# Gated GELU on one core: blocks of 16 rows with one packed store in place of tiles of 8 rows

## The chip, the cores and the metric

The kernel runs on one core of a Trainium2 chip. The metric is the device time of one execution in microseconds; the median of three runs before the change is 469.12 us (469.11 to 469.23). The profile is of one further execution, whose span from the first to the last instruction is 467.9 us.

## The reference

```python
def reference(x):                       # x: (32, 512, 2048) float32
    half_dim = x.shape[-1] // 2
    x1, x2 = x[..., :half_dim], x[..., half_dim:]
    gelu_x1 = 0.5 * x1 * (1 + erf(x1 / np.sqrt(2)))
    return (gelu_x1 * x2).astype(np.float32)
```

There are 16,384 rows. Each is 8 KB in and 4 KB out: 134.22 MB are read and 67.11 MB are written.

## The kernel before

The rows are cut into 16 tiles of 1024 rows. A tile gives every one of the 128 partitions 8 consecutive rows (R = 8), so that a partition's part is 64 KB of input that lies together in memory and 32 KB of output that lies together. Two input buffers (`x0_tile`, `x1_tile`, 64 KB per partition each) and two output buffers (`o0_tile`, `o1_tile`, 32 KB each) alternate by tile: tile i uses number i % 2.

Four engines take part, each with a program of its own, in order:
- SyncE (SP) issues the loads (`load`, L47). Three are issued ahead: tile 0 in two pieces of four rows and tile 1 whole. In the loop it waits until tile i is multiplied (L108) and then issues the load of tile i + 2 into the buffer that tile i has left (L109).
- ScalarE (ACT) waits for the tile (L79), applies GELU to the first halves of the rows (L81) into the output buffer, and issues the store (`store`, L51, the DMA at L54) after a wait for the multiply. The store goes into ScalarE's own DMA queue (q10); the loads go into SyncE's (q1).
- VectorE (DVE) multiplies the output buffer by the second halves of the rows, in place (L89).
- GpSimd sets four constants at the start, TensorE does nothing.

A full tile is computed in two steps of 5 and 3 rows; the first and the last tile in steps of 2, 2 and 4 rows, with a store for each four rows. The semaphore `ready[k]` counts both the load and the store of buffer pair k: ScalarE starts tile i + 2 when the load of it has landed and the store of tile i has as well. The last three stores (tile 14, and two halves of tile 15) go through SyncE's queue, behind the last load. At the end the semaphores are cleared, and SyncE waits for the last stores.

A DMA's work is shared by 16 DMA engines. Transfers of one queue are taken in order; the two queues are served by the same 16 engines.

Of the kernel before, what the change touches and what calls it, by code (L numbers as in the profile page):

```python
# [1 line left out]

# [4 lines left out]

GELU = mybir.ActivationFunctionType.Gelu


@with_exitstack
def kernel(
    ctx: ExitStack,
    tc: tile.TileContext,
    x: bass.AP,
    out: bass.AP,
):
    nc = tc.nc
    P = nc.NUM_PARTITIONS

    x_flat = x.flatten_outer_dims()
    out_flat = out.flatten_outer_dims()
    n_rows, dim = x_flat.shape
    half = dim // 2

    R = 8
    x_t = x_flat.rearrange("(n p r) d -> n p r d", p=P, r=R)
    o_t = out_flat.rearrange("(n p r) d -> n p r d", p=P, r=R)
    n_tiles = x_t.shape[0]
    x_bufs = [nc.alloc_sbuf_tensor(f"x{k}_tile", [P, R, dim], x.dtype) for k in range(2)]  # L30
    o_bufs = [nc.alloc_sbuf_tensor(f"o{k}_tile", [P, R, half], out.dtype) for k in range(2)]

    first = [nc.alloc_semaphore(f"first{j}") for j in range(2)]
    ready = [nc.alloc_semaphore(f"ready{k}") for k in range(2)]
    gelu_done = nc.alloc_semaphore("gelu_done")
    mul_done = nc.alloc_semaphore("mul_done")
    tail_stored = nc.alloc_semaphore("tail_stored")
    n = {sem.name: 0 for sem in [*first, *ready, gelu_done, mul_done, tail_stored]}  # L40

    def counted(ins, sem, by):
        ins.then_inc(sem, by)
        n[sem.name] += by

    def load(i, rows, sem):
        ins = nc.sync.dma_start(out=x_bufs[i % 2][:, rows, :], in_=x_t[i][:, rows, :])  # L47
        counted(ins, sem, 16)
        return ins

    def store(queue, i, rows, sem):  # L51
        queue.wait_ge(mul_done, n[mul_done.name])
        counted(
            queue.dma_start(out=o_t[i][:, rows, :], in_=o_bufs[i % 2][:, rows, :]), sem, 16  # L54
        )

    for ins in (  # L60
        load(0, slice(0, 4), first[0]),
        load(0, slice(4, 8), first[1]),
        load(1, slice(0, 8), ready[1]),
    ):
        tc.no_tile_sem_insts.add(ins.ins.name)
    tc.close()
    tc.compile()  # L67

    for i in range(n_tiles):
        k = i % 2  # L70
        last = i == n_tiles - 1
        pieces = i == 0 or last
        steps = ((0, 2), (2, 4), (4, 8)) if pieces else ((0, 5), (5, 8))
        for lo, hi in steps:
            rows = slice(lo, hi)
            if i == 0 and lo % 4 == 0:
                nc.scalar.wait_ge(first[lo // 4], 16)
            elif lo == 0:
                nc.scalar.wait_ge(ready[k], n[ready[k].name])  # L79
            counted(  # L80
                nc.scalar.activation(  # L81
                    out=o_bufs[k][:, rows, :], in_=x_bufs[k][:, rows, :half], func=GELU
                ),
                gelu_done,
                1,
            )
            nc.vector.wait_ge(gelu_done, n[gelu_done.name])
            counted(
                nc.vector.tensor_mul(  # L89
                    out=o_bufs[k][:, rows, :],  # L90
                    in0=o_bufs[k][:, rows, :],
                    in1=x_bufs[k][:, rows, half:],
                ),
                mul_done,
                1,
            )
            if pieces and hi % 4 == 0:
                if last:
                    store(nc.sync, i, slice(hi - 4, hi), tail_stored)
                else:  # L100
                    store(nc.scalar, i, slice(hi - 4, hi), ready[k])
        if not pieces:
            if i == n_tiles - 2:
                store(nc.sync, i, slice(0, R), tail_stored)
            else:
                store(nc.scalar, i, slice(0, R), ready[k])
        if i + 2 < n_tiles:
            nc.sync.wait_ge(mul_done, n[mul_done.name])  # L108
            load(i + 2, slice(0, R), ready[k])  # L109


    nc.scalar.drain()  # L112
    for sem in (*first, *ready):
        nc.scalar.sem_clear(sem)
    nc.vector.drain()
    nc.vector.sem_clear(gelu_done)
    nc.sync.sem_clear(mul_done)
    nc.sync.wait_ge(tail_stored, n[tail_stored.name]).then_inc(
        tail_stored, -n[tail_stored.name]
    )  # L120


# [1 line left out]
_INS = ['x']  # L124
_OUTS = [((32, 512, 1024), 'float32')]


# [23 lines left out]
```

## Time and profile before

| what | value |
|---|---|
| median of three runs | 469.12 us |
| span of the profiled execution | 467.9 us |
| VectorE busy, 34 multiplies | 140.5 us (30%) |
| ScalarE busy, 34 GELUs and a table load | 115.5 us (25%) |
| GELU of 5 rows (128x5120), 3 rows (128x3072) | 4.47 us, 2.75 us |
| multiply of 5 rows, 3 rows | 5.49 us, 3.35 us |
| mean rate of the DMA over the span | 430 GB/s |

The page's row of DMA shares divides the span into 40 slices of 11.7 us; a digit is the share in tenths in which the 16 engines were busy in a slice. The DMA section counts packets, megabytes and the share of the engines' time for each queue; q1 is SyncE's, q10 ScalarE's. "DMA issues" gives the median time from issue to landing, which includes the time that a transfer stands in its queue. The chain of waits is followed back from the last instruction: at each step to the work that released it. Windows are stretches of the span, in microseconds from its start, for which the packets that begin in them are counted.

### The profile page before, as it was taken

Reading aid. Unit: us, or ns where it says so; the run is one execution under the profiler, and the core shown is the slowest. Engines: PE = TensorE matmul, PEld = TensorE weight load, DVE = VectorE, ACT = ScalarE, POOL = GpSimd, SP = SyncE. Lnnn points to the kernel's source line nnn. Section 1 sums busy time; section 2 is a strip of 40 time slices with the busy share of each in tenths; the row PEclk is TensorE's granted clock in tenths of the full one; section 3 lists DMA queues with packets and bytes.
Section 4 is the critical chain, followed back from the end, with each engine's and each line's share of the span. In section 5 each row is a group of like instructions: output and inputs, shape, how many; then the busy total and the mean of one; then the engine's idle time right before and its main releaser. Section 6 shows DMA issues by size and latency. Waiting matters only on the chain.

```text
span 467.9 us, 152 instructions
## 1 busy us (share of the span) xinstructions
DVE 140.5 (30%) x34; ACT 115.5 (25%) x35; POOL 0.2 (0%) x4
## 2 busy tenths in 40 slices
DVE  0330514207052060511606116060150702507043
ACT  1320606042060410604106050050500506014060
POOL 0000000000000000000000000000000000000000
DMA  8999999999999999999999999999999999999998
GB/s 359 448 448 443 403 405 492 409 403 448 459 437 403 434 417 493 403 403 448 476 420 403 445 406 493 403 406 445 487 409 403 445 451 448 403 434 417 493 389 373
DMA packets 5041, 201.34 MB, mean 430 GB/s; under 512 B 560, under 2 KB 560, under 8 KB 560
## 3 DMA queue, kind: packets, MB, share of 16 engines
q1 hardware_dynamic: 2880, 142.61, 70.6%
q10 hardware_dynamic: 2160, 58.72, 29.1%
q14 instruction: 1, 0.01, 0.0%
HBM read 134.22 MB, written 67.11 MB: 430 GB/s over the span
## 4 chain that ended last, share of the span: by engine, by line
DMA 76%; DVE 14%; ACT 8%; ACTq 0%; SPq 0%; issue 0%
DMA out_dram<-o_tile 66%; DVE o_tile L89 14%; DMA x_tile<-in_x_dram 10%; ACT o_tile L81 8%; ACTq L112 0%; SPq L47 0%
## 5 line engine op out<-in xcount | busy, mean ns | idle before, releaser
L89 DVE TENSOR_TENSOR o_tile<-o_tile,x_tile 128x5120 f32<-128x5120 f32 (+3 forms) x34 | 140.5, 4171 | 319.7 <-ACT o_tile L81 319.7
L81 ACT ACTIVATE o_tile<-x_tile 128x5120 f32<-128x5120 f32 (+3 forms) x34 | 114.3, 3407 | 337.4 <-DMA out_dram<-o_tile 301.6
L81 ACT ACT_TABLE_LOAD x1 | 1.3, 1283 | 2.9 <-PEq L67 2.9
L135 POOL MEMSET const-bfloat16-1.0<- 128x1 bf16 x1 | 0.1, 101 | 0.0
L135 POOL MEMSET const-uint8-127<- 128x1 uint8 x1 | 0.1, 101 | 0.0
L135 POOL MEMSET const-float32-0.0<- 128x1 f32 x1 | 0.1, 98 | 0.2 <-issue 0.2
L135 POOL MEMSET const-float32-1.0<- 128x1 f32 x1 | 0.1, 98 | 0.0
## 6 DMA issues: line engine op xcount, KB each, us to landing
out_dram<-o_tile ACTq DMA_DIRECT2D x13, 4096.0 KB, 44.7
x_tile<-in_x_dram SPq DMA_DIRECT2D x2, 4096.0 KB, 16.6
out_dram<-o_tile ACTq DMA_DIRECT2D x2, 2048.0 KB, 34.5
out_dram<-o_tile SPq DMA_DIRECT2D x1, 4096.0 KB, 25.2
out_dram<-o_tile SPq DMA_DIRECT2D x2, 2048.0 KB, 7.8
x_tile<-in_x_dram SPq DMA_DIRECT2D x15, 44.2
```

What stands on the lines that cost most here:

```text
L81: nc.scalar.activation(out=o_bufs[k][:, rows, :], in_=x_bufs[k][:, rows, :half], func=GELU),
L89: nc.vector.tensor_mul(out=o_bufs[k][:, rows, :], in0=o_bufs[k][:, rows, :], in1=x_bufs[k][:, rows, half:],),
L135: nc = _bacc.Bacc("TRN2", target_bir_lowering=False, num_devices=1)
```

## The change

The unit of work becomes a block of 16 rows per partition, in two halves of 8 rows; there are 8 blocks. For a partition, a half is one load of 64 KB, and the block's output is one store of 64 KB.

There are three buffers of 64 KB per partition in place of four. The first halves alternate in `x0_tile` and `x1_tile` (`buffer_of`), all second halves use `x2_tile`. GELU is computed in place in the input buffer. The multiply writes packed rows of 4 KB into the first half's buffer: the results of the first half into its lower 32 KB, those of the second half into its upper 32 KB. VectorE waits for its own previous multiply before each one.

The order of the loads: (0,0), (0,1) and (1,0) are issued ahead, all whole. When block b is multiplied, ScalarE issues its store and SyncE issues load (b+1, 1) into `x2_tile`. Then SyncE waits until the store of block b has landed (`stored`) and issues load (b+2, 0) into the buffer that was stored. The semaphores `landed` count loads only. All halves are computed in steps of 5 and 3 rows, except for the very last, which keeps 2, 2 and 4. The last block is stored in three pieces through SyncE's queue: 8 rows, 4 rows, 4 rows. There are 16 loads and 10 stores where there were 17 and 18.

```diff
-    x_t = x_flat.rearrange("(n p r) d -> n p r d", p=P, r=R)
-    o_t = out_flat.rearrange("(n p r) d -> n p r d", p=P, r=R)
-    x_bufs = [nc.alloc_sbuf_tensor(f"x{k}_tile", [P, R, dim], x.dtype) for k in range(2)]
-    o_bufs = [nc.alloc_sbuf_tensor(f"o{k}_tile", [P, R, half], out.dtype) for k in range(2)]
+    x_t = x_flat.rearrange("(n p h r) d -> n h p r d", p=P, r=R, h=2)
+    o_t = out_flat.rearrange("(n p r) d -> n p r d", p=P, r=2 * R)
+    bufs = [nc.alloc_sbuf_tensor(f"x{k}_tile", [P, R * dim], x.dtype) for k in range(3)]
...
+    def buffer_of(b, h):
+        return 2 if h else b % 2
+
+    def load(b, h):
+        k = buffer_of(b, h)
+        dst = bufs[k][:, :].rearrange("p (r d) -> p r d", r=R)
+        return counted(nc.sync.dma_start(out=dst, in_=x_t[b, h]), landed[k], 16)
+
+    def packed(b, lo, hi):
+        rows = bufs[b % 2][:, lo * half : hi * half]
+        return rows.rearrange("p (r d) -> p r d", d=half)
+
+    def store(queue, b, lo, hi, sem):
         queue.wait_ge(mul_done, n[mul_done.name])
+        counted(queue.dma_start(out=o_t[b][:, lo:hi, :], in_=packed(b, lo, hi)), sem, 16)
+
+    def compute(b, h, lo, hi):
+        src = bufs[buffer_of(b, h)][:, lo * dim : hi * dim]
+        src = src.rearrange("p (r d) -> p r d", d=dim)
         counted(
+            nc.scalar.activation(out=src[:, :, :half], in_=src[:, :, :half], func=GELU),
+            gelu_done,
+            1,
+        )
+        if n[mul_done.name]:
+            nc.vector.wait_ge(mul_done, n[mul_done.name])
+        nc.vector.wait_ge(gelu_done, n[gelu_done.name])
+        counted(
+            nc.vector.tensor_mul(
+                out=packed(b, h * R + lo, h * R + hi),
+                in0=src[:, :, :half],
+                in1=src[:, :, half:],
+            ),
+            mul_done,
+            1,
         )
...
+    for ins in (load(0, 0), load(0, 1), load(1, 0)):
         tc.no_tile_sem_insts.add(ins.ins.name)
...
+    for b in range(n_blocks):
+        last = b == n_blocks - 1
+        for h in range(2):
+            k = buffer_of(b, h)
+            waited[k] += 16
+            nc.scalar.wait_ge(landed[k], waited[k])
+            if last and h:
+                for lo, hi in ((0, 2), (2, 4), (4, 8)):
+                    compute(b, h, lo, hi)
+                    if hi % 4 == 0:
+                        store(nc.sync, b, R + hi - 4, R + hi, tail_stored)
+            else:
+                for lo, hi in ((0, 5), (5, 8)):
+                    compute(b, h, lo, hi)
                 if last:
+                    store(nc.sync, b, 0, R, tail_stored)
+        if last:
+            continue
+        store(nc.scalar, b, 0, 2 * R, stored[b % 2])
+        nc.sync.wait_ge(mul_done, n[mul_done.name])
+        load(b + 1, 1)
+        if b + 2 < n_blocks:
+            nc.sync.wait_ge(stored[b % 2], n[stored[b % 2].name])
+            load(b + 2, 0)
...
+    for sem in stored:
+        nc.sync.wait_ge(sem, n[sem.name])
+        nc.sync.sem_clear(sem)
```

## The prediction

> **What bounds the kernel now.** I read the page first: the row of DMA shares, then the packet counts and the two queues.
>
> ```profile
> DMA  8999999999999999999999999999999999999998
> ...
> DMA packets 5041, 201.34 MB, mean 430 GB/s; under 512 B 560, under 2 KB 560, under 8 KB 560
> ...
> q1 hardware_dynamic: 2880, 142.61, 70.6%
> q10 hardware_dynamic: 2160, 58.72, 29.1%
> ```
>
> The 16 DMA engines are busy for 70.6 + 29.1 = 99.7% of the span. VectorE (30%) and ScalarE (25%) are far from it. The counts say how a transfer is cut. q1 is SyncE's queue and holds 20 transfers (17 loads, 3 stores at the end); 2880 / 20 = 144 packets: 128 with data, one per partition, and 16 small ones. q10 is ScalarE's: 15 stores, 2160 / 15 = 144. A full load is 8.39 MB, so its packets are 64 KB; a full store's are 32 KB.
>
> Next the chain that ended last, in order of time, for one tile of the steady part:
>
> ```profile
> 100.56 4.48 ACT o_tile L81
> ...
> 105.06 8.77 DVE o_tile L89 x2
> ...
> 113.85 44.68 DMA out_dram<-o_tile
> ...
> 158.56 4.48 ACT o_tile L81
> ```
>
> The same buffer comes round every 158.56 - 100.56 = 58.00 us, in which two tiles move 2 x 12.58 MB: 433.9 GB/s. So 8.39 MB alone takes 19.33 us and a 64 KB packet, 1/8 of it on each engine, 2.42 us. From landing to issue the chain takes 13.3 us (4.48 + 8.77 + handovers); the DMA does not notice, since the other buffer's load and store are queued.
>
> The issues show how the two queues share an engine:
>
> ```profile
> out_dram<-o_tile ACTq DMA_DIRECT2D x13, 4096.0 KB, 44.7
> ...
> x_tile<-in_x_dram SPq DMA_DIRECT2D x15, 44.2
> ```
>
> A store of half the bytes, issued with a load, lands with it. So the queues take turns packet by packet, 32 KB against 64 KB.
>
> Last, how soon a queue that was empty is served. The first load's issue starts at 0.73 (timeline); up to 1.73 no packet has run, up to 2.31 all 16 engines have their first: 1.0 to 1.6 us. The first store is issued at 19.23:
>
> ```profile
> 19.23 0.38 ACTq L54 DMA_DIRECT2D out_dram<-o_tile  x1
> ```
>
> Packets in the window 19.2 to 24.3, then in 19.2 to 25.05:
>
> ```profile
> DMA packets 63, 2.06 MB, mean 405 GB/s; under 512 B 16, under 2 KB 16, under 8 KB 16
> ...
> q1 hardware_dynamic: 63, 2.06, 99.1%
> ```
>
> ```profile
> q1 hardware_dynamic: 66, 2.26, 94.5%
> q10 hardware_dynamic: 16, 0.26, 10.4%
> ```
>
> For 5 us only loads run. If the store was visible after 1.0 to 1.6 us (20.2 to 20.8), then beside the packet in progress each engine still passed the load's small packet (all 16 lie between 21.58 and 22.08) and one whole packet of the next load. I read this as about two packets committed ahead. It is the reading that decides this case.
>
> **The change, part by part.**
>
> *Fewer packets.* 35 transfers become 26, so each engine handles 81 packets fewer (9 each). The first half-load, 8 packets of 32 KB, took 22.46 - 12.76 = 9.70 us between landings; six times that is 58.20, with 54 packets against the 36 of a 58.00 us period for the same bytes: 0.20 / 18 = 0.011 us a packet at most, given rounding. 81 x 0.011 = 0.9; the other end is 0. I take 0.4 us gained.
>
> *Start.* The two 32 KB-row loads of tile 0 become one, and the early GELU at 12.76 moves to 22.46. Cost 0: three 8.39 MB loads stand in SyncE's queue and keep the engines busy until 22.08 + 2 x 19.33 = 60.7. Without that cover it would cost the 9.7 us.
>
> *Compute.* In-place GELU with a strided output, packed multiply: strided input is there already (5120 columns 4.47 us, VectorE 5.49). I take 0; the other bound is VectorE's 23% higher time for its strided form, some 3 us on 13.3. VectorE's new wait on its own last multiply loses the overlap of the pair, 5.49 + 3.35 - 8.77 = 0.07, about 0.1 us. Both lie under the load in flight (below).
>
> *Tail.* From the last landing, 448.56, to the end, 19.3 us: same three stores, same queue, same pieces. Two waits of SyncE on `stored` precede its last wait and lie under the last store. Cost 0.
>
> *The moved load.* SyncE now waits for `stored[b % 2]` before the load of the next first half, and before the multiply wait and load behind it. Call X the first-half load in flight, S the block's store, Y the second-half load issued with S, Z the first-half load that waits for S. ScalarE's own queue holds nothing urgent: the next GELU needs X. Block 0 from the rows:
> - Load (0,0) seen 22.46; (0,1) at 41.8; S and Y issued at 41.8 + 13.4 = 55.2. X's packets end at 60.2 to 60.7, so on the first engine its seventh runs 55.4 to 57.8, its eighth to 60.2.
> - S is visible at 56.2 to 56.8, in the seventh packet. With two packets committed, the eighth and X's small one pass; S starts at 60.2.
> - S and Y have 8 packets each, now of one size, and alternate: both end at 60.2 + 16 x 2.42 = 98.9. Then **both queues are empty**, and Z is issued only when S is seen.
>
> The price of an empty queue: the first load took 12.0 us from issue to landing, of which 4.19 MB account for 9.67: 2.35 us of overhead. With the 0.02 us handover, 2.37 us idle.
>
> Block 1: Y seen at 99.75, S and Y issued 113.1. Z, now X, started late and has its last packets end at 120.6; at 114.1 its sixth packet runs, the seventh and eighth are committed, S comes before X's small packet, which takes a turn. So Y has one packet, 2.42 us, left when S's small packet goes. Z needs 0.4 to be seen by the last engine, up to 0.5 of spread, 1.0 to its first packet: 1.9 to 2.0. No idle time. Z follows Y directly, as in block 0. So the gap comes at every second handover: 3 of the 6 (Z exists for blocks 0 to 5).
>
> Sum against the profiled execution: 467.9 - 0.4 + 3 x 2.37 = 474.6 us. The median lies 1.2 us above the span (469.12), so 475.8.
>
> A rule against this reading: the Trainium skill, "DMA: Bandwidth & Descriptors", section "Queues, rings and completion order", says that an engine drains a whole packet, typically 9 to 17 descriptors, before it turns to the other queue. An engine's share of a transfer here is 9 pieces, so by the rule S would run whole between X and Y, Z would find Y still queued, and the time would be 468.7. The trace disagrees: between 131 and 157.5 us q1 ran 112 packets and q10 122, interleaved, and the store lands with the load.
>
> **Rivals.**
> 1. *No idle time: 467.5 + 1.2 = 468.7 us, not slower.* If S takes its turn right after X's seventh or eighth packet, as the 1.0 to 1.6 us of the first load would have it, one or two packets of Y (2.4 to 4.8 us) are left at each handover, over the 2.0 needed. It decides as soon as fewer than two packets are committed ahead. For it: the first store is one event, and on a queue that had never run. Against it: all 16 engines show those 5 us alike.
> 2. *A gap at all six handovers: 467.5 + 6 x 2.37 = 481.7, median 482.9.* It takes one more committed packet, or a chain from landing to issue longer by a packet (the 3 us bound on compute). For it: the margin in odd blocks is only 2.42 - 2.0 = 0.4 us. Against it: with a third packet committed the first store would have come one packet later than it did if it was visible at 20.8, and the compute forms hardly differ.
> 3. *The larger store packets speed the transfers up.* At the most 0.9 us: 467.0 + 1.2 = 468.2. The queues already run at 433.9 GB/s; there is nothing else to win.
>
> **How the numbers follow.** Forecast (three gaps) 0.38, all six 0.21, none 0.36 with the 0.9 us end in it, other slow phases between them 0.05. A difference under 0.2% (0.9 us) can't be told from none here. Slower: 0.38 + 0.21 + 0.05 = 0.64; within: 0.34; faster: 0.02, only the upper end of the packet gain. Time 475.8. The forecast's own range is 474 to 478 (gap 1.9 to 3 us each); for 8 in 10 it must reach the no-gap case below, 468.4, and the six-gap case above, 483.5.
>
> **What would show it.** Right: DMA digits of 7 or 8 in the slices around 99, 217 and 336 us (2.4 us of 11.9), and GB/s near 350 there; q1 2736 packets, q10 1008. A small packet of a store that comes with the small packet of Y means gap; ahead of Y's last data packet means none. All nines: rival 1. Six dips: rival 2. Wrong altogether if the GELU or multiply rows grow by more than 1 us, or if 1:1 phases run off 434 GB/s.

## The result, and the profile after

The median of six runs is 492.47 us against 469.28 us for the kernel before: 4.9% longer. The runs of the kernel after spread from 486.5 to 497.4 us where those before stay within 0.3 us; the ratio with its interval, 1.0439 (1.0408 to 1.0470), compares only runs near a kernel's fastest and so lies below that of the medians. The profiled execution took 493.68 us, with a span of 492.4 us: 24.5 us more than before. The forecast was 475.8 us, with 468.4 to 483.5 as the range: the direction was right, the size under a third of what came.

The page of the kernel after, the same rows as before, and the issues:

```profile
DMA  9999999999999999999999999999999999999978
...
DMA packets 3745, 201.34 MB, mean 409 GB/s; under 512 B 416, under 2 KB 416, under 8 KB 416
...
q1 hardware_dynamic: 2736, 142.61, 70.4%
q10 hardware_dynamic: 1008, 58.72, 27.8%
...
x_tile<-in_x_dram SPq DMA_DIRECT2D x16, 43.4
out_dram<-x_tile ACTq DMA_DIRECT2D x7, 43.9
```

The packet counts are those worked out. But the digits hide the loss: the engines are busy for 70.4 + 27.8 = 98.2% of a span that is 24.5 us longer, and move 409 GB/s in place of 430. 98.2% of 492.4 us is 17.0 us more busy time than 99.7% of 467.9 us. So most of the lost time is not idle time of the DMA engines; it is packets that take longer.

Windows from one start of the second half's GELU to the next, one per block, then the end. The columns are the stretch, its length, VectorE's, ScalarE's and GpSimd's busy time, the clock, the DMA share and GB/s:

```profile
41.86:101.57 59.71, 17.70 (x4) 14.24 (x4) 0.00 (x0) 1.00 1.00 421
101.57:161.66 60.09, 17.70 (x4) 14.24 (x4) 0.00 (x0) 1.00 0.99 419
161.66:221.74 60.08, 17.70 (x4) 14.25 (x5) 0.00 (x0) 1.00 1.00 418
221.74:282.27 60.53, 17.70 (x4) 14.24 (x4) 0.00 (x0) 1.00 0.99 417
282.27:342.70 60.43, 17.70 (x4) 14.24 (x5) 0.00 (x0) 1.00 0.99 415
342.70:404.43 61.73, 17.70 (x4) 14.24 (x4) 0.00 (x0) 1.00 0.99 415
404.43:472.96 68.53, 17.70 (x4) 14.25 (x5) 0.00 (x0) 1.00 0.97 380
472.96:492.40 19.44, 9.01 (x3) 7.21 (x3) 0.00 (x0) 1.00 0.74 314
```

At the pace of the kernel before, a block would take 58.0 us. Six blocks together lose 14.6 us (1.7 to 3.7 each), the seventh 10.5 us. The start (41.86, worked out as 41.8) and the end (19.44 against 19.3) cost nothing, as forecast. Without these losses, which are 25.1 us, the span would be 41.86 + 7 x 58.0 + 19.44 = 467.3 us, 0.6 us less than before the change.

Now the packets around the first store of block 0, issued at 55.35. Four windows of the kernel after, in order of time: 55.4 to 56.0, 57.8 to 58.45, 61.3 to 62.2 and 63.5 to 64.6. The last number is the time of the packets that begin there, as a share of 16 engines' window, so that share x length x 16 / packets is the mean time of one.

```profile
q1 hardware_dynamic: 16, 1.05, 406.1%
```

```profile
q1 hardware_dynamic: 16, 1.05, 548.1%
```

```profile
q10 hardware_dynamic: 16, 1.05, 268.7%
```

```profile
q10 hardware_dynamic: 16, 1.05, 220.0%
q1 hardware_dynamic: 16, 0.00, 0.8%
```

The load's seventh packet takes 4.061 x 0.60 = 2.44 us, its eighth 5.481 x 0.65 = 3.56 us: 1.14 us more than the 2.42 of a steady packet, on all 16 engines at once. The stores' packets take 2.42 us again. And the order is not the one worked out: the first store packet (61.3 to 62.2) comes before the load's small one (63.5 to 64.6).

At the other end of that store, the window 97.5 to 99.9:

```profile
q1 hardware_dynamic: 16, 1.05, 100.8%
q10 hardware_dynamic: 16, 0.00, 0.4%
```

The store's small packets run here, and so does one more 64 KB packet of the load Y on every engine. So the store ends while Y still has a packet: the load queue is not empty at block 0. Z follows with little delay, but its start is slow too: the window 100.3 to 101.6 holds 13 data packets that take 2.84 us each (1.777 x 1.3 x 16 / 13).

```profile
q1 hardware_dynamic: 22, 0.85, 177.7%
```

Both places are slow in all of the first six blocks. At the third store, issued at 175.15, the window 177.1 to 178.3 has the load's eighth packets:

```profile
q1 hardware_dynamic: 16, 1.05, 320.7%
```

3.207 x 1.2 = 3.85 us. At the other four stores they take 3.6 to 3.9 us, worked out in the same way; over six stores this is some 7.8 us more than 2.42 each. Z's first packets take 2.8 to 3.2 us in all six blocks, together some 3.5 us more. That is 11.3 of the 14.6 us, and little of the loss is idle time. The whole window from 41.86 to 404.43 has

```profile
q1 hardware_dynamic: 1734, 101.06, 67.5%
q10 hardware_dynamic: 864, 50.33, 32.0%
```

so the engines are busy for 99.5% of it and idle for 1.8 of 362.6 us.

### The profile page after: what moved, and what is told of

Its sections match the earlier page's. It is cut to its first block, busy times and chain, and to the rows that moved or that the text cites. A ratio compares the mean times of both kernels' runs of the same rounds, so it can differ in the third digit from the quotient of the medians.

```text
span 492.4 us, 174 instructions
## 1 busy us (share of the span) xinstructions
DVE 141.8 (29%) x33; ACT 115.3 (23%) x34; POOL 0.2 (0%) x4
## 3 DMA queue, kind: packets, MB, share of 16 engines
q1 hardware_dynamic: 2736, 142.61, 70.4%
q10 hardware_dynamic: 1008, 58.72, 27.8%
## 4 chain that ended last, share of the span: by engine, by line
DMA 70%; DVE 12%; ACT 8%; another core or an unknown queue 8%; ACTq 0%; issue 0%; SPq 0%; DVEq 0%
DMA x_tile<-in_x_dram 61%; DVE x_tile L80 12%; DMA out_dram<-x_tile 9%; ACT x_tile L72 8%; ACTq L120 0%; SPq L58 0%; DVEq L78 0%
## 5 line engine op out<-in xcount | busy, mean ns | idle before, releaser
L80 DVE TENSOR_TENSOR x_tile<-x_tile 128x5120 f32<-128x5120 f32 (+3 forms) x33 | 141.8, 4296 | 342.9 <-ACT x_tile L72 342.4
L72 ACT ACTIVATE x_tile<-x_tile 128x5120 f32<-128x5120 f32 (+3 forms) x33 | 114.1, 3505 | 362.0 <-DMA x_tile<-in_x_dram 362.0
```

The source lines that it names most:

```text
L72: nc.scalar.activation(out=src[:, :, :half], in_=src[:, :, :half], func=GELU),
L80: nc.vector.tensor_mul(out=packed(b, h * R + lo, h * R + hi), in0=src[:, :, :half], in1=src[:, :, half:],),
```

## The experiments

The expectations weigh five readings of the loss and call them theories. Layout: the new addresses or the larger store packets are slow by themselves. Restart: each store that starts on an empty queue costs about half a packet. Handover: time is lost only where a load waits for a store. Equal-packet: loads and stores with packets of one size run badly together. Depth: the load queue holds too little when a load has to wait. The code shown is shortened.

**Is it the layout of the rows in memory?** The kernel before, with the kernel after's addresses:

```diff
-    x_t = x_flat.rearrange("(n p r) d -> n p r d", p=P, r=R)
+    x_t = x_flat.rearrange("(n p h r) d -> n h p r d", p=P, r=R, h=2)   # out_flat too; tile i is [i // 2, i % 2]
```

> The kernel before with the rows laid out as in the kernel after: two tiles share a block of 16 rows per partition, so loads have 64 KB packets at 128 KB pitch and stores 32 KB packets at 64 KB pitch; all else as before. Layout theory: a good part of the 23 us, over 480 us. Restart and handover theories: as before, 469 us within 1.

Measured: 469.29 us, ratio 1.0001 (0.9989 to 1.0012). This layout, with the store packets still of 32 KB, costs nothing.

**Does each start of a store on an empty queue cost its half packet?** Three kernels with transfers alone, all with loads queued two deep and never waiting for a store. The stores go out together, or each behind a landed load, or each behind it and cut in two:

```diff
+    nc.sync.wait_ge(landed[where(j)], ...)   # the load that was last in this buffer
+    load(j)
...
+    for b in range(n_blocks):
+        nc.scalar.wait_ge(landed[1], 16 * b)   # left out with the full queue
+        nc.scalar.dma_start(out=o_t[b], in_=first_buffer)   # in two halves in the third kernel
```

> Transfers alone, the same bytes: 16 loads of 64 KB packets in a row, always two queued, and 8 stores of 64 KB packets of one buffer, issued together, so that the store queue starts once and never runs empty before its end (GELU and multiply are left out, the stores write the first half of the input's first block). Restart theory (each store that starts on an empty queue costs 1.2 to 1.5 us): one start, about 468 us. Layout theory (64 KB packets at 128 KB pitch, or 64 KB against 64 KB, are slower by themselves): over 480 us. Handover theory (time is lost only where the load waits for the store): no such wait here, about 467 us.

> The same transfers, but store b is issued when load 2b has landed, so that each of the 8 stores starts on an empty queue beside a running load; the loads still never wait for a store. Restart theory: 8 starts of 1.2 to 1.5 us against one, 8 to 11 us over the run with the full queue, 476 to 479 us, and in each start one load packet per engine of some 3.6 us in place of 2.42. Handover theory: no load waits for a store, so the same as the full queue within 1 us. Layout theory: the same as the full queue, and that over 480 us.

> As the run with a start per block, but each store is cut into two of 32 KB packets, issued one after the other. Packet by packet against 64 KB loads they last 16 x 3.63 = 58 us, the whole block, so the queue hardly runs empty. Restart theory: close to the full queue, under 471 us. Handover theory: the same as the other two. A theory that it is the number of stores issued that costs: as slow as the run with a start per block or slower.

Measured: 473.17, 473.09 and 479.72 us. The restart theory falls: eight starts cost no more than one. In the second run the load packet ahead of the store is long at the first store (window 24.0 to 24.6: 5.559 x 0.6 = 3.34 us), but not at the second, in the window 82.9 to 83.7:

```profile
q1 hardware_dynamic: 16, 1.05, 302.5%
```

3.025 x 0.8 = 2.42 us. The level, 3.8 us above the kernel before, was foreseen by none of the theories. The third run was expected to be the best of the starts and is the slowest; why was not settled. What counts for the case is the second: with store packets of 64 KB, a fresh start in every block and 201.33 MB, but with two loads always queued, 19 of the 23 us are gone. These runs compute nothing and have no load that waits for a store, so they do not say which wait costs.

**Which buffer is missing?** The three buffers of the kernel after were halved (R = 4, packets of 32 KB, 16 blocks), which leaves room to vary their number:

```diff
-    R = 8
+    R = 4
+    F, S = 2, 1        # 3, 1; 2, 2; 3, 2: first-half and second-half buffers
...
-        return 2 if h else b % 2
+        return F + b % S if h else b % F
...
-        load(b + 1, 1)
+        load(b + S, 1)      # and load(b + F, 0) behind the wait for the store
```

> The kernel after at half the size: 4 rows a half, 16 blocks of 8 rows, packets of 32 KB, still two first-half buffers and one second-half buffer. Depth theory (time is lost where the load queue holds too little: its loads wait for the store and for the multiply, and the fixed delays of an issue do not shrink with the packets): 15 block borders at 2 us or more each, over 495 us. Equal-packet theory (store packets as large as the load packets take turns one to one and run badly by themselves): near the kernel after's loss of 23 us or half of it, 480 to 492 us.

> The same with a third first-half buffer, so that the load that waits for a store is issued a block earlier; the second halves still share one buffer. If the wait for the store is what costs (the place named in the prediction): 470 to 475 us. If the wait of the second-half load for the multiply costs as much: about half of the loss of the run with two and one stays. Equal-packet theory: 480 to 492 us.

> The same with two first-half buffers and a second second-half buffer: the second-half load no longer stands right behind the multiply, the first-half load still waits for the store, but with another load queued ahead of it. If the wait for the store costs whatever is queued: over 490 us. Depth theory: 470 to 478 us. Equal-packet theory: 480 to 492 us.

> Three first-half and two second-half buffers: both waits have a block of slack, packets of loads and stores are still of one size and the store queue still runs empty in each block. Depth theory: 468 to 473 us. Equal-packet theory: 480 to 492 us, no better than the others. A theory that each start of a store on an empty queue costs half a packet (0.6 us here): 15 x 0.6 = 9 us, 477 us.

Measured: 517.25, 521.10, 481.41 and 481.62 us. A second second-half buffer brings 36 us. The third first-half buffer brings nothing, with one second-half buffer or with two. But it does not test the wait for the store: SyncE's program still waits for a store in every block (320.5 us in 13 waits with three and one), and the added first-half load only stands in front of the second-half load that the chain needs. What tells is that the wait for the store stays almost as long with two second-half buffers. SyncE's waits for stores in the run with two and one, then with two and two (total, number, longest):

```profile
SPq L59 <- DMA out_dram<-x_tile: 345.1, 14, 24.9
```

```profile
SPq L59 <- DMA out_dram<-x_tile: 331.9, 14, 24.4
```

The 36 us are gone all the same. So the wait for the store does not cost this by itself; what costs is the *second-half* load, which waits for the multiply with too little queued ahead of it. Windows of the run with two and one, then with two and two:

```profile
60.00:120.00 60.00, 14.23 (x7) 13.62 (x8) 0.00 (x0) 1.00 0.95 384
120.00:180.00 60.00, 17.86 (x8) 12.34 (x7) 0.00 (x0) 1.00 0.99 406
180.00:240.00 60.00, 18.33 (x8) 14.84 (x8) 0.00 (x0) 1.00 0.96 388
```

```profile
60.00:120.00 60.00, 18.34 (x8) 14.62 (x8) 0.00 (x0) 1.00 1.00 431
120.00:180.00 60.00, 18.33 (x8) 14.62 (x8) 0.00 (x0) 1.00 1.00 425
180.00:240.00 60.00, 18.34 (x8) 14.62 (x8) 0.00 (x0) 1.00 1.01 432
```

With one second-half buffer, engines stand idle (a share of 0.95) and busy ones are slow; with two, the rate is nearly that of the kernel before. Several expectations were missed. The run with three and one was to take 470 to 475 us, or to lose about half; it lost no less. The depth theory's 470 to 478 us and 468 to 473 us for two second-half buffers were too low by 3 and 9 us, and both times lie in the 480 to 492 us of the equal-packet theory. That theory cannot be the whole, as it gave the same range for the runs that took 517 and 521 us; for the 12 us that remain it is not excluded. They go with a mean of some 425 GB/s in the middle; why is open.

**Is it the time from landing to issue?** If the load queue is too short, less work between a landing and the next issue must help as a buffer does, with the buffers and the wait for the store as they are. No compute at all, and GELU without the multiply:

```diff
# no compute at all
-                    compute(b, h, lo, hi)
...
-        nc.sync.wait_ge(mul_done, n[mul_done.name])
+        nc.sync.wait_ge(landed[2], 16 * (b + 1))
...
# GELU alone
-            gelu_done,
+            mul_done,
             1,
         )
-        nc.vector.wait_ge(gelu_done, n[gelu_done.name])
-        counted(nc.vector.tensor_mul(...), mul_done, 1)
```

> The transfers of the kernel after with its buffers and its order, but no GELU and no multiply: store b and load (b+1, 1) are issued when load (b, 1) has landed, load (b+2, 0) still waits for store b (the last block is one store, behind its landing, so some 2 us of the end are its own). Depth theory (the 13.3 us from landing to issue use up the one load that stands in the queue): 470 to 475 us. Theory that the wait of the first-half load for the store costs by itself, as the prediction had it: over 485 us.

> The kernel after without the multiply (the second halves are not used): 7.1 us from landing to issue in place of 13.3, all waits otherwise as they were. Depth theory: most of the loss gone, as more than 5 of the 8 packets of the load in flight are still to run when the next is issued, 470 to 480 us. Theory that the wait for the store costs by itself: over 485 us.

Measured: 477.01 us, above the 470 to 475 us of the depth theory (some 2 us are its own end, an estimate), and 478.22 us. Both are far below 485: with GELU alone the second block's issue follows its landing by 7.15 us (101.86 to 109.01) in place of 13.5, and those 6.3 us, at seven block borders, gain 14 us in all, although VectorE is busy for 29% of the span only. The 14 us hold the slow block too: in the profile with GELU alone seven blocks take from 41.90 to 456.06, 8.2 us more than 7 x 58.0 in place of 25.1 us, and none is slow (after the first, two together take 117.8 to 118.3).

In the run with GELU alone the second store is issued at 109.02. The packet ahead of it is there the load's sixth, with two more to follow, and not the eighth. The load packets that begin in the window 112.0 to 113.0:

```profile
q1 hardware_dynamic: 15, 0.98, 226.8%
```

2.268 x 1.0 x 16 / 15 = 2.42 us: the last load packet ahead of the store is not lengthened. In the kernel after, at the second store, the window 117.5 to 118.2 has

```profile
q1 hardware_dynamic: 15, 0.98, 493.9%
```

4.939 x 0.7 x 16 / 15 = 3.69 us. The lengthening goes with the short load queue, not with the start of a store as such. The fit is not complete. At the first store of the run with GELU alone, the 16 load packets that begin between 50 and 52 us took 3.44 us too, as in the transfers alone. And at its last store, issued at 404.14, the packets in the window 405.3 to 406.4, the load's sixth and seventh, take 3.010 x 1.1 = 3.31 us:

```profile
q1 hardware_dynamic: 16, 1.05, 301.0%
```

**The same with all the work done.** The second half in two pieces of four rows, each loaded, computed and given back by itself:

```diff
+        for part in range(2):
+            nc.scalar.wait_ge(landed[2 + part], 16 * (b + 1))
+            compute(b, 1, 4 * part, 4 * part + 4)
+            nc.sync.wait_ge(mul_done, n[mul_done.name])
+            load(b + 1, 1, part)
```

> The kernel after with all its work, but the second half is loaded, computed and its buffer given back in two pieces of 4 rows (32 KB packets): the first piece's load is issued some 4 us ahead of the store and the last piece's multiply ends 8 us after the landing instead of 13.3. Depth theory: 470 to 482 us. Theory that the wait for the store costs by itself: over 485 us.

Measured: median 480.22 us of nine runs, from 471.1 to 483.6; ratio 1.0099 (1.0054 to 1.0144), formed as in the section on the result. Without another byte of buffer half of the loss goes, by the medians. It is still not faster than the kernel before, and no version here is: that kernel's engines are busy for 99.7% of the span.

**Where does the 68 us block come from?** The kernel after, unchanged, for a second trace.

> The kernel after once more, for a second trace: 486 to 497 us; blocks 60 us apart instead of 58. If the 68 us of the last block but one come from its place in the program (the last stores in the load queue), they come again there; if from engines that have drifted apart, somewhere else or not at all.

Measured: 493.87 us. Its windows by block, the same columns:

```profile
42.10:102.02 59.92, 17.70 (x4) 14.25 (x5) 0.00 (x0) 1.00 1.00 419
102.02:162.18 60.16, 17.70 (x4) 14.24 (x4) 0.00 (x0) 1.00 1.00 419
162.18:223.01 60.83, 17.70 (x4) 14.25 (x4) 0.00 (x0) 1.00 0.99 412
223.01:284.66 61.65, 17.70 (x4) 14.25 (x5) 0.00 (x0) 1.00 0.99 418
284.66:352.70 68.04, 17.70 (x4) 14.24 (x5) 0.00 (x0) 1.00 0.90 348
352.70:414.75 62.05, 17.70 (x4) 14.25 (x5) 0.00 (x0) 1.00 1.01 422
414.75:474.01 59.26, 17.70 (x4) 14.24 (x4) 0.00 (x0) 1.00 0.98 424
```

The long block comes two blocks earlier, so it does not belong to the place in the program or to the last stores. In both traces the blocks grow slowly ahead of it. In the first trace, inside the long block, the windows show busy engines that move little:

```profile
431.00:441.00 10.00, 8.39 (x2) 4.12 (x2) 0.00 (x0) 1.00 1.02 361
441.00:451.00 10.00, 0.46 (x1) 0.00 (x0) 0.00 (x0) 1.00 0.91 341
```

In the second trace the long block has idle time too (a share of 0.90). Both fit engines that have drifted apart, so that loads on some run beside stores on others, and a landing waits for the last of them.

The drift itself can be read from the traces, as a load ends with one small packet on each engine. In the kernel before, the 16 of the last load begin between 447.45 and 448.05. In the kernel after, those of load (1,1) begin between 99.95 and 101.35, those of load (7,1), with which the long block ends, between 462.4 and 472.2. In the second trace they lie between 343.1 and 352.4 at the end of the long block and between 379.7 and 380.5 in the next. So the engines are apart in both long blocks. But the drift is not enough: with GELU alone the small packets of one load lie between 413.6 and 426.8, and no block is long. No run here sets the drift by itself, and the cause of the long block stays open.

## Why the prediction was wrong

*Right:* the bound (DMA), the counts (2736 and 1008 packets), the start, the end, the compute forms (GELU 4.48 us; the multiplies 5.50 and 3.37 us, now one after the other), the time of the first issue (55.35 against 55.2), and that the store starts when X's eighth packet has run.

*The order of the packets* failed first: "the eighth and X's small one pass; S starts at 60.2". The store's first packet came ahead of X's small packet, so one packet was committed, not two, if the store was visible in the seventh as worked out. It follows as under rival 1 that Y has a packet left when the store ends, and the sum's term "3 x 2.37" does not exist in this form. What is left of it is Z's slow first packet, some 0.4 us in block 0, and the DMA share of the first six blocks is 0.99 to 1.00 where the gaps of the forecast would have taken it to 0.96 in every second one. Rival 1 had this order of the packets right, and its 468.7 us wrong, as it too counted idle time alone.

*The step that failed for the size* is that the whole price of the moved load was counted as idle time, "3 x 2.37". "Both lie under the load in flight" took a covered wait to be free. The load in flight did cover the 13.5 us: over the six blocks the engines are idle for some 1.8 us only. But the six blocks lose 14.6 us, largely with the engines busy: some 7.8 us in the load's last packet ahead of the stores (3.6 to 3.9 us in place of 2.42), some 3.5 us in Z's first packets; the other 3.3 us, with the idle time in them, were not traced further. The sum has no term for either. And the multiply on the path from landing to issue, priced at 0 as long as the load in flight lasts, turned out to be worth 14 us, the slow block included.

*The place.* The forecast put the whole price on the first-half load behind `stored`. Its six handovers cost some 3.5 us in place of 7.1, and more is lost at the issue behind the multiply. The runs at half size with two second-half buffers and those with less compute kept the wait for the store and lost far less time. So the greater part hangs on the second-half load behind the multiply, through the one buffer that all second halves share. A kernel of full size and with all the work, but without the wait for the store, was not run.

*Not foreseen at all:* the one slow block, 10.5 us in the first trace of the kernel and 10.0 us in the second, and perhaps with it the spread of 11 us between runs. Rival 2's 482.9 us came nearer by luck: its six gaps of idle time are not there either.

## What to carry to other kernels

In a kernel bound by its transfers, count for each queue what is still to run at the moment the next transfer is issued, and keep a further transfer there; a queue that is merely never empty was not enough here. How little would have done was not measured. The buffer that was saved by sharing was paid for by the chain from landing through compute to reissue, though the engines of that chain are idle most of the time. The 0.6 us between 467.9 and 467.3 is all that shows for nine transfers fewer; a load queue that falls to two packets cost some 2 us in every block.

## What the runs showed of the hardware

- Beside a short load queue, the load's last packet ahead of a store takes 3.56 to 3.91 us in place of 2.42, at each of the first six stores of the kernel after. With more of the load to follow, the second store of the run with GELU alone left it at 2.42 us. At a run's first store it was long with more to follow too (3.44 us there, 3.34 us in the transfers alone). Why is open.
- The small packet that ends a transfer takes its own turn in its queue, behind a packet of the other one (61.3 to 64.6 us above).
- The DMA share can read 1.02 at 361 GB/s: busy engines are no proof of the full rate, 434 GB/s here. The GB/s has to be read beside it.
- Eight stores of 64 KB packets beside a deep load queue (473.1 us) run within 1% of the kernel before; with the stores cut into 32 KB packets the same transfers take 6.6 us longer. Why was not settled.
- The 16 DMA engines can drift apart: the ends of one load lie within 0.6 us in the kernel before, and up to some 9.7 us apart in the kernel after. Why, and why they come together again, is open.
